# Strassen's seven block products for the second MLP product of a two-layer trunk on one core

## The chip, the cores and the metric

The kernel runs on one NeuronCore of a Trainium2 chip. Five engines work side by side, each through its own queue in order: PE (TensorE, matrix products into PSUM), DVE (VectorE), ACT (ScalarE), POOL (GpSimd) and SP (SyncE, which here issues every DMA). SBUF is the working memory of 128 partitions, PSUM holds eight banks of 128x512 float32 for the results of PE, DRAM holds inputs and spilled tensors. The metric is the device time of one execution in microseconds (us).

## The reference, cut to what matters

Two layers of a trunk over 1024 tokens with 1024 channels, in float32. Each layer has a token mixer, an output projection, and then an MLP with a hidden width of 4096:

```python
def sqrelu_mlp(h, w1, w2):
    return jnp.square(jax.nn.relu(h @ w1)) @ w2

for layer in range(2):
    h = rms_norm(x, norm_mix[layer])
    ...                                   # token mixer and memory attention
    x = x + jnp.concatenate([y_mix, y_mem], axis=-1) @ w_out[layer]
    x = x + sqrelu_mlp(rms_norm(x, norm_mlp[layer]), w_mlp_in[layer], w_mlp_out[layer])
```

The second MLP product is `hidden (1024x4096) @ w_mlp_out (4096x1024)`, added to the residual x.

## The kernel before

Everything is held transposed: channels on the partitions, tokens along the free axis, split into two halves `h` of 512 tokens. Each float32 operand of a product is split into a rounded part `hi` and a remainder `lo` (type float32r), and a product of 128x128 by 128x512 is three matmuls, hi·hi, hi·lo and lo·hi (`t3`). A weight block of 128x1024 is loaded by a DMA into one of two buffers `wr`, copied by ACT to `wh` (L242) and its remainder `wl` made by DVE or POOL (L244); there are three buffers each of `wh` and `wl`, and `wnext` prepares the plan's entries up to two ahead of the one in use.

The MLP of a layer is `mlp`. `mlp_z(m, hs)` makes 128 hidden channels for both token halves: 24 matmuls into a PSUM bank of tag `pj` (2 banks) by way of `mmq` (L269), then relu and scale on DVE (L849), the square's rounded part on ACT (L851), the square on POOL (L852) and its remainder on DVE (L853). The second product goes in eight groups `g` of four hidden blocks: for each of 8 output blocks `dm` and 2 halves, 12 matmuls (4 hidden blocks of three) into a `pj` bank by way of `mm` (L264), and one addition of that bank on DVE to the residual tile `x[h][dm]`, which stays in SBUF over the whole MLP (L900). A group so has 16 results of 12 matmuls, 192, and beside it stand 8 results of 24 matmuls, 192, for the next group's hidden blocks. In the last group of layer 0, x is also stored to DRAM (`xs`, in the profile `xspill`), squared and summed for the next norm (`sqacc`, L322 and L328), and its first half split for the next layer (`split`, L333 and L334). In the last group of layer 1 the tiles go to `out`; the very last tile is done in two halves of 256.

SBUF is shared out by hand: `R` has 58 tiles of 128x512 for split operands, `F` has 25 tiles of 128x515 for everything in float32; both hand out the tile that has been free the longest. The order of the instructions on each engine is not that of the code: a scheduler of the language orders them when the program is built.

Of the kernel before, what the change touches and what calls it, by code (L numbers as in the profile page):

```python
# [139 lines left out]
class Builder:  # L140
    NR = 58
    NF = 25
# [3 lines left out]
    def __init__(self, ctx, tc, ins, out):  # L146
# [24 lines left out]
        self.plan = []  # L171
        self.wpos = self.wload = self.wrawn = 0
# [7 lines left out]
        self.hid = {}  # L180
# [5 lines left out]
        self.x = [None, None]  # L186
# [36 lines left out]

    def _wraw(self, upto):
        while self.wrawn < min(len(self.plan), upto):
            i = self.wrawn
            buf, src, n = self._wbuf(i, self.wraw), self.plan[i][0], self.plan[i][1]
            for s in (slice(0, n // 2), slice(n // 2, n)) if i == 0 else (slice(0, n),):
                self.nc.sync.dma_start(buf[:, s], src[:, s])
            self.wrawn += 1  # L230

    def _wsplit(self, upto):
        nc = self.nc
        while self.wload < min(len(self.plan), upto):
            i = self.wload
            self._wraw(i + 1)
            n = self.plan[i][1]
            parts = self.plan[i][2]
            raw, hi, lo = (self._wbuf(i, b) for b in (self.wraw, self.whi, self.wlo))
            for q in range(parts):  # L240
                s = slice(q * n // parts, (q + 1) * n // parts)
                nc.scalar.activation(hi[:, s], raw[:, s], AF.Copy)  # L242
                eng = nc.gpsimd if q in self.pool_parts else nc.vector
                eng.tensor_tensor(lo[:, s], raw[:, s], hi[:, s].bitcast(F32), ALU.subtract)  # L244
            self.wload += 1
            self._wraw(self.wload + 2)
# [497 lines left out]
    def outproj(self, h, ks, src, dst, gain, last):  # L744
        nc = self.nc
        if last and gain is not None:
            self.xg[h] = []
            self.x[h] = []
        for m in range(8):
# [14 lines left out]
            if last and gain is not None:  # L764
                self.xg[h].append(self.split(xv, self.pc(gain, m)))
                self.x[h].append(x)
            else:
                self.F.put(x)
# [4 lines left out]
    def outproj2(self, h, k0, k1, src, gain, side):  # L773
# [26 lines left out]
        self.x[h] = []  # L800
        for m in range(8):
# [7 lines left out]
            self.sqacc(m, h, xv, nc.vector)  # L809
            self.xg[h].append(self.split(xv, self.pc(gain, m)))  # L810
            self.x[h].append(x)
# [10 lines left out]

    def plan_mlp(self, l, nz, nw):
        w1 = [(self.ins["w1"][l * 32 + m], 1024, 1) for m in range(32)]
        w2 = [(self.ins["w2"][l * 32 + i], 1024, 1) for i in range(32)]
        self.plan += w1[nz:nz + nw] + w1[0:4]
        for g in range(8):
            self.plan += w1[4 * (g + 1):4 * (g + 1) + 2]
            self.plan += w2[4 * g:4 * g + 4]
            self.plan += w1[4 * (g + 1) + 2:4 * (g + 2)]  # L830

    def mlp_z(self, m, hs, hook=None):
        nc = self.nc
        wh, wl = self.wnext()
        for h in hs:
            if (m, h) in self.hid:
# [13 lines left out]
            hi, lo = self.R.get(), self.R.get()  # L850
            nc.scalar.activation(hi, r[:, n], AF.Square)  # L851
            nc.gpsimd.tensor_tensor(r[:, n], r[:, n], r[:, n], ALU.mult)  # L852
            nc.vector.tensor_tensor(lo, r[:, n], hi.bitcast(F32), ALU.subtract)  # L853
            self.F.put(r)
            self.hid[(m, h)] = (hi, lo)
# [5 lines left out]

    def mlp(self, l, src, nz, nw, nxt=None):
        nc = self.nc
        hid = self.hid
# [8 lines left out]
        self.x[0] = [self.load_x(k, 0, src) for k in range(8)]  # L873
        for g in range(8):
            if g < 7:
                for m in range(4 * g + 4, 4 * g + 6):
                    drain(self.mlp_z(m, (0, 1)))
# [7 lines left out]
            for c in range(4):  # L885
                wh, wl = self.wnext()
                for d in range(2):
                    dm = 2 * c + d
                    for h in range(2):
                        end = l == 1 and g == 7 and dm == 7 and h == 1  # L890
# [546 lines left out]
```

## Time and profile before

| | |
|---|---|
| three runs | 2275.31, 2278.61, 2284.72 us (median 2278.61) |
| the profiled execution's own time | 2282.31 us |
| its span, first to last instruction | 2280.6 us |
| mean granted TensorE clock | 0.988 |
| matmuls in the profile | 11058 |
| DMA over the span | 181.84 MB, mean 80 GB/s |

The profile is of one execution. A busy share is the time in which an engine had at least one instruction under way; matmuls overlap each other, so the time of one matmul row (395 ns) is longer than the pace at which they follow. "idle before" in a group's row is the time that the engine stood still just before such instructions, with what ended it.

### The profile page before, as it was taken

Reading aid. Unit: us, or ns where it says so; the run is one execution under the profiler, and the core shown is the slowest. Engines: PE = TensorE matmul, PEld = TensorE weight load, DVE = VectorE, ACT = ScalarE, POOL = GpSimd, SP = SyncE. Lnnn points to the kernel's source line nnn. Section 1 sums busy time; section 2 is a strip of 40 time slices with the busy share of each in tenths; the row PEclk is TensorE's granted clock in tenths of the full one; section 3 lists DMA queues with packets and bytes.
Section 4 is the critical chain, followed back from the end, with each engine's and each line's share of the span. In section 5 each row is a group of like instructions: output and inputs, shape, how many; then the busy total and the mean of one; then the engine's idle time right before and its main releaser. Section 6 shows DMA issues by size and latency. Waiting matters only on the chain.

```text
span 2280.6 us, 28820 instructions
## 1 busy us (share of the span) xinstructions
PE 2223.7 (98%) x11058; PEld 1852.9 (81%) x11058; DVE 1215.5 (53%) x2320; ACT 754.0 (33%) x1500; POOL 491.3 (22%) x504
## 2 busy tenths in 40 slices
PE   8889999999999999999999998999999999999999
PEld 6788777888888888888998996778788888888887
DVE  8988864333333333346677778887433333333332
ACT  5755642111111111124556756764211111111110
POOL 3743601110110110102133543321110110101100
PEclk9999999999999999999999998999999999999999
DMA  5422353111111111214335221564211111111112
GB/s 176 119 63 74 116 158 101 47 47 51 50 47 47 47 47 47 61 51 139 112 103 163 89 80 28 171 190 135 77 52 47 47 47 47 46 47 46 47 47 83
DMA packets 69785, 181.84 MB, mean 80 GB/s; under 512 B 7888, under 2 KB 10256, under 8 KB 69648
## 3 DMA queue, kind: packets, MB, share of 16 engines
q1 hardware_dynamic: 69648, 180.01, 25.9%
q8 instruction: 87, 1.43, 0.3%
q14 instruction: 50, 0.41, 0.1%
HBM read 162.12 MB, written 17.86 MB: 79 GB/s over the span
## 4 chain that ended last, share of the span: by engine, by line
PE 83%; DVE 9%; DMA 4%; ACT 2%; issue 2%; POOL 1%; SPq 0%; DVEq 0%; ACTq 0%; POOLq 0%
PE pspj L269 43%; PE pspj L264 31%; DVE wl L244 1%; DMA f<-xspill 1%; DMA xspill<-f 1%; PE pss L1072 1%; ACT f L209 1%; PE pss L264 1%; PE pspt L789 1%; PE pso L577 1%; PE pspt L1114 1%; DVE f L1077 1%; DVE r L340 1%; PE pspt L269 0%; PE pspj L789 0%
## 5 line engine op out<-in xcount | busy, mean ns | idle before, releaser
L269 PE MATMUL pspj<-r,wh 128*128 128x512 f32 x2656 | 849.8, 400 | 18.0 <-DVE f L759 9.7
L264 PE MATMUL pspj<-r,wh 128*128 128x512 f32 (+1 forms) x2056 | 644.2, 395 | 0.3 <-DVE f L900 0.3
L269 PEld LDWEIGHTS pspj<-r,wh 128*128 128x128 f32 x2656 | 499.2, 189 | 140.8 <-issue 7.7
L242 ACT ACTIVATE wh<-wr 128x256 fp32r<-128x256 f32 (+3 forms) x433 | 276.6, 669 | 905.9 <-PE pspj L264 421.9
L269 PE MATMUL pspj<-r,wl 128*128 128x512 f32 x1328 | 527.6, 397 | 0.0
L264 PEld LDWEIGHTS pspj<-r,wh 128*128 128x128 f32 x2056 | 385.3, 188 | 93.2 <-DVE f L900 0.8
L852 POOL TENSOR_TENSOR f<-f 128x512 f32<-128x512 f32 x128 | 166.9, 1304 | 1254.7 <-ACT r L851 1254.7
L264 PE MATMUL pspj<-r,wl 128*128 128x512 f32 (+1 forms) x1028 | 405.2, 394 | 0.0
L900 DVE TENSOR_TENSOR f<-f,pspj 128x512 f32<-128x512 f32 (+1 forms) x257 | 175.7, 684 | 422.6 <-PE pspj L264 422.5
L244 DVE TENSOR_TENSOR wl<-wr,wh 128x1024 fp32r<-128x1024 f32 (+3 forms) x322 | 287.4, 902 | 59.8 <-ACT wh L242 57.8
L269 PEld LDWEIGHTS pspj<-r,wl 128*128 128x128 f32 x1328 | 251.2, 189 | 60.3 <-issue 0.2
L269 PE MATMUL pspj<-wh,r 128*128 128x256 f32 (+1 forms) x1408 | 275.6, 289 | 5.7 <-DVE r L981 2.3
L849 DVE SCALAR_TENSOR_TENSOR f<-pspj,f 128x512 f32<-128x512 f32 x128 | 88.4, 691 | 282.0 <-PE pspj L269 279.5
L269 PEld LDWEIGHTS pspj<-wh,r 128*128 128x128 f32 x1408 | 226.7, 193 | 8.7 <-DVE r L981 2.6
L264 PEld LDWEIGHTS pspj<-r,wl 128*128 128x128 f32 x1028 | 193.1, 188 | 46.9
L269 PE MATMUL pspj<-wl,r 128*128 128x256 f32 (+1 forms) x704 | 201.8, 287 | 6.3 <-DVE wl L244 6.3
L851 ACT ACTIVATE r<-f 128x512 fp32r<-128x512 f32 x128 | 79.8, 624 | 289.4 <-DVE f L849 289.4
L853 DVE TENSOR_TENSOR r<-f,r 128x512 fp32r<-128x512 f32 x128 | 89.2, 697 | 149.5 <-POOL f L852 149.5
L269 PEld LDWEIGHTS pspj<-wl,r 128*128 128x128 f32 x704 | 135.6, 193 | 7.7 <-DVE wl L244 6.8
L244 POOL TENSOR_TENSOR wl<-wr,wh 128x256 fp32r<-128x256 f32 (+2 forms) x111 | 91.6, 849 | 123.4 <-ACT wh L242 115.7
L1089 POOL TENSOR_SCALAR f<-f,frc 128x512 f32<-128x512 f32 (+2 forms) x96 | 63.6, 672 | 150.2 <-DVE frc L1087 99.1
L209 ACT ACTIVATE f<-f,mn 128x512 f32<-128x512 f32 (+2 forms) x96 | 58.4, 611 | 31.4 <-DVE mn L1077 28.8
(246 smaller groups left out, 1987.9 us busy)
## 6 DMA issues: line engine op xcount, KB each, us to landing
wr<-in_w_dram SPq DMA_DIRECT2D x134, 512.0 KB, 3.6
f<-xspill SPq DMA_DIRECT2D x72, 256.0 KB, 3.6
xspill<-f SPq DMA_DIRECT2D x48, 256.0 KB, 2.2
f<-in_xT_dram SPq DMA_DIRECT2D x32, 256.0 KB, 3.5
wr<-in_wkv_dram SPq DMA_DIRECT2D x16, 512.0 KB, 3.7
wr<-in_wina_dram SPq DMA_DIRECT2D x15, 512.0 KB, 3.9
f<-cscr SPq DMA_DIRECT2D x24, 256.0 KB, 4.1
wr<-in_wxqa_dram SPq DMA_DIRECT2D x8, 512.0 KB, 3.7
```

The source lines that it names most:

```text
L209: i = self.nc.scalar.activation(*a, **k)
L242: nc.scalar.activation(hi[:, s], raw[:, s], AF.Copy)
L244: eng.tensor_tensor(lo[:, s], raw[:, s], hi[:, s].bitcast(F32), ALU.subtract)
L264: self.nc.tensor.matmul(out, lhsT=a, rhs=b, start=(j == 0), stop=(j == n - 1))
L269: self.nc.tensor.matmul(out, lhsT=a, rhs=b, start=(j == 0), stop=(j == n - 1))
L340: self.nc.vector.tensor_tensor(lo[:, :n], src, hi[:, :n].bitcast(F32), ALU.subtract)
L849: nc.vector.scalar_tensor_tensor(r[:, n], ps, 0.0, self.rsb[h][:, n], ALU.max, ALU.mult)
L851: nc.scalar.activation(hi, r[:, n], AF.Square)
L852: nc.gpsimd.tensor_tensor(r[:, n], r[:, n], r[:, n], ALU.mult)
L853: nc.vector.tensor_tensor(lo, r[:, n], hi.bitcast(F32), ALU.subtract)
L900: nc.vector.tensor_tensor(x, x, ps[:, cs], ALU.add)
L1089: nc.gpsimd.tensor_scalar(s[:, :n], s[:, :n], rc, 0.0, ALU.mult, ALU.add)
```

## The change

The second MLP product is cut into pairs: two output blocks by two hidden blocks by two token halves. Such a 2x2x2 piece has eight block products; in Strassen's form it has seven, p1 to p7, of sums and differences of blocks. The hidden blocks' sums (t1 to t4) are made by `hid_parts` in SBUF and all seven operands split into hi and lo; the weights' sums are made on POOL while the weight block is prepared, in two plan entries `s1` (blocks p1, p2, p6, p5) and `s2` (p7, p3, p4). Each product runs over the two pairs of a group, 6 matmuls to a PSUM bank, and `mlp_out` brings the seven banks together to four residual tiles. The residual tiles no longer stay in SBUF: they are loaded from `xspill` for each pair of output blocks in each group (`acc_load`) and stored again (`sink`), and the output projections ahead of the MLPs store x there too. `R` has 60 tiles and `F` 23. The weights of `w_mlp_out` are laid out by blocks on the host.

```diff
-    NR = 58
-    NF = 25
+    NR = 60
+    NF = 23
...
+    def _wpart(self, hi, lo, raw, eng):
+        self.nc.scalar.activation(hi, raw, AF.Copy)
+        eng.tensor_tensor(lo, raw, hi.bitcast(F32), ALU.subtract)
...
+                if parts == "s1":
+                    self.wx = f
+                    G.tensor_tensor(f[:, q:2 * q], a21, a22, ALU.add)
+                    G.tensor_tensor(f[:, 0:q], f[:, q:2 * q], a11, ALU.subtract)
+                    self._wpart(hi[:, 0:512], lo[:, 0:512], raw[:, 0:512], nc.vector)
+                    self._wpart(hi[:, 512:1024], lo[:, 512:1024], f[:, 0:512], nc.vector)
+                else:
+                    G.tensor_tensor(f[:, 0:q], a11, a21, ALU.subtract)
+                    G.tensor_tensor(f[:, q:2 * q], a12, self.wx[:, 0:q], ALU.subtract)
+                    self._wpart(hi[:, 512:768], lo[:, 512:768], a22, nc.vector)
+                    self._wpart(hi[:, 0:512], lo[:, 0:512], f[:, 0:512], nc.vector)
...
-            hi, lo = self.R.get(), self.R.get()
-            nc.scalar.activation(hi, r[:, n], AF.Square)
             nc.gpsimd.tensor_tensor(r[:, n], r[:, n], r[:, n], ALU.mult)
-            nc.vector.tensor_tensor(lo, r[:, n], hi.bitcast(F32), ALU.subtract)
-            self.F.put(r)
-            self.hid[(m, h)] = (hi, lo)
+            self.zz[(m, h)] = r
...
+    def hid_parts(self, m):
...
+        p["b11"] = self.split_sb(b11)
+        V.tensor_tensor(b11, b12, b11, ALU.subtract)
+        p["t1"] = self.split_sb(b11)
+        p["b21"] = self.split_sb(b21)
+        p["b22"] = self.split_sb(b22)
+        V.tensor_tensor(b12, b22, b12, ALU.subtract)
+        p["t3"] = self.split_sb(b12)
+        V.tensor_tensor(b11, b22, b11, ALU.subtract)
+        p["t2"] = self.split_sb(b11)
+        V.tensor_tensor(b21, b21, b11, ALU.subtract)
+        p["t4"] = self.split_sb(b21)
...
+    def acc_load(self, q):
+        return {(a, b): self.load_x(2 * q + a, b, self.xs) for a in range(2) for b in range(2)}
...
+        def sink(a, b):
+            f = acc[(a, b)]
+            x, dm = f[:, n], 2 * q + a
+            if g == 7 and l == 1:
+                nc.sync.dma_start(self.out[dm, :, b * H:(b + 1) * H], x)
+            else:
+                nc.sync.dma_start(self.xs[dm, :, b * H:(b + 1) * H], x)
+            if g == 7 and l == 0:
+                self.sqacc(dm, b, x, V if b == 0 else None)
+                if b == 0:
+                    self.xg[0].append(self.split(x, self.pc("gmix1", dm)))
+            self.F.put(f)
+
+        for q in range(4):
...
+            p1 = self.psum("pj")
+            prod(p1, 0, w, "b11")
+            nc.scalar.activation(t, p1, AF.Copy)
+            V.tensor_tensor(c11, c11, p1, ALU.add)
+            p2 = self.psum("pj")
+            prod(p2, 1, w, "b21")
+            V.tensor_tensor(c11, c11, p2, ALU.add)
+            sink(0, 0)
+            p6 = self.psum("pt")
+            prod(p6, 2, w, "t2")
+            V.tensor_tensor(t, t, p6, ALU.add)
+            p5 = self.psum("s")
+            prod(p5, 3, w, "t1")
+            V.tensor_tensor(u, t, p5, ALU.add)
+            G.tensor_tensor(c12, c12, u, ALU.add)
+            G.tensor_tensor(c22, c22, u, ALU.add)
...
+            p7 = self.psum("s")
+            prod(p7, 0, w, "t3")
+            V.tensor_tensor(t, t, p7, ALU.add)
+            V.tensor_tensor(c22, c22, p7, ALU.add)
+            G.tensor_tensor(c21, c21, t, ALU.add)
...
+            p3 = self.psum("pt")
+            prod(p3, 1, w, "b22")
+            V.tensor_tensor(c12, c12, p3, ALU.add)
+            sink(0, 1)
+            sink(1, 1)
+            p4 = self.psum("pt")
+            prod(p4, 2, w, "t4")
+            V.tensor_tensor(c21, c21, p4, ALU.add)
+            sink(1, 0)
...
         for g in range(8):
+            if g:
+                parts = []
+                for m in range(4 * g + 1, 4 * g + 4):
+                    drain(self.mlp_z(m, (0, 1)))
+                    if m % 2:
+                        parts.append(self.hid_parts(m - 1))
+            acc = self.acc_load(0)
             if g < 7:
-                for m in range(4 * g + 4, 4 * g + 6):
-                    drain(self.mlp_z(m, (0, 1)))
+                drain(self.mlp_z(4 * g + 4, (0, 1)))
...
-                        for cs in (slice(0, 256), slice(256, 512)) if end else (slice(0, H),):
-                            ps = self.psum("pj")
-                            terms = []
-                            for kk in range(4):
-                                s = slice(kk * M + d * P, kk * M + (d + 1) * P)
-                                a, b = hid[(4 * g + kk, h)]
-                                terms += self.t3(wh[:, s], wl[:, s], a[:, cs], b[:, cs])
-                            self.mm(ps[:, cs], terms)
-                            x = self.x[h][dm][:, cs]
-                            nc.vector.tensor_tensor(x, x, ps[:, cs], ALU.add)
+            self.mlp_out(l, g, parts, acc)
```

Because a scheduler sets the order, two places are shown on DVE. The first is in the middle of an MLP, where one group's second product ends and the next hidden blocks begin. Before, L900 is the addition of a bank, L244 a weight remainder, L849 and L853 belong to the hidden blocks:

```order
L900 TENSOR_TENSOR f_130<-f_130,pspj_4754 128x512
L900 TENSOR_TENSOR f_126<-f_126,pspj_4768 128x512
L900 TENSOR_TENSOR f_125<-f_125,pspj_4782 128x512
L900 TENSOR_TENSOR f_139<-f_139,pspj_4796 128x512
L244 TENSOR_TENSOR wl_154<-wr_149,wh_151 128x1024
L849 SCALAR_TENSOR_TENSOR f_148<-pspj_4813,f_132 128x512
```

Now the same place holds the eight additions of seven banks (L949 and L952 for p1 and p2, L956 for p6, L959 for p5, L967 and L968 for p7, L973 for p3, L978 for p4), the weight remainder (L246), and `hid_parts` of the next group (L372 a remainder, L896 a difference):

```order
L372 TENSOR_TENSOR r_123<-f_128,r_122 128x512
L949 TENSOR_TENSOR f_127<-f_127,pspj_5013 128x512
L896 TENSOR_TENSOR f_128<-f_139,f_128 128x512
L952 TENSOR_TENSOR f_127<-f_127,pspj_5022 128x512
L956 TENSOR_TENSOR f_132<-f_132,pspt_5031 128x512
L372 TENSOR_TENSOR r_83<-f_128,r_82 128x512
L959 TENSOR_TENSOR f_131<-f_132,pss_5039 128x512
L246 TENSOR_TENSOR wl_155<-wr_149,wh_152 128x1024
L967 TENSOR_TENSOR f_132<-f_132,pss_5052 128x512
L973 TENSOR_TENSOR f_142<-f_142,pspt_5062 128x512
L968 TENSOR_TENSOR f_130<-f_130,pss_5052 128x512
L978 TENSOR_TENSOR f_135<-f_135,pspt_5072 128x512
```

Between two additions of banks now stand instructions that read two tiles of SBUF, and the banks have three tags (`pj`, `pt`, `ps` with tag `s`) in place of one.

The second place is the last group of layer 0, where the residual is also prepared for the next layer. Before, on DVE (L328 adds squares, L334 splits x for layer 1):

```order
L900 TENSOR_TENSOR f_135<-f_135,pspj_7095 128x512
L244 TENSOR_TENSOR wl_155<-wr_150,wh_152 128x256 x2
L900 TENSOR_TENSOR f_130<-f_130,pspj_7121 128x512
L328 TENSOR_TENSOR f_145<-f_145,f_132 128x512
L334 SCALAR_TENSOR_TENSOR r_91<-f_130,par,r_90 128x512
L900 TENSOR_TENSOR f_126<-f_126,pspj_7140 128x512
```

Now (L360 adds squares, L366 splits x):

```order
L978 TENSOR_TENSOR f_129<-f_129,pspt_7776 128x512
L246 TENSOR_TENSOR wl_156<-wr_149,wh_153 128x256
L360 TENSOR_TENSOR f_126<-f_126,f_136 128x512
L973 TENSOR_TENSOR f_138<-f_138,pspt_7856 128x512
L967 TENSOR_TENSOR f_133<-f_133,pss_7846 128x512
L366 SCALAR_TENSOR_TENSOR r_93<-f_129,par,r_92 128x512
L360 TENSOR_TENSOR f_126<-f_126,f_127 128x512
L246 TENSOR_TENSOR wl_154<-wr_150,wh_151 128x512
L968 TENSOR_TENSOR f_143<-f_143,pss_7846 128x512
L949 TENSOR_TENSOR f_140<-f_140,pspj_7890 128x512
L956 TENSOR_TENSOR f_141<-f_141,pspt_7912 128x512
```

The additions of the squares and the splits stand between additions of banks on which the next products wait for a free bank.

More of the change, by code (lines that the diff above doesn't have):

```diff
@@ L222, in _wbuf, with _wridx, _wrawbuf @@
         return bufs[i % len(bufs)][:, :self.plan[i][1]]
+    def _wridx(self, i):
+        while len(self.ridx) <= i:
+            e = self.plan[len(self.ridx)]
+            self.nraw += e[0] is not None
+            self.ridx.append(self.nraw - 1)
+        return self.ridx[i]
+    def _wrawbuf(self, i):
+        return self.wraw[self._wridx(i) % len(self.wraw)]
     def _wraw(self, upto):
@@ new lines, in acc_load, with mlp_out, prod @@
+    def acc_load(self, q):
+        return {(a, b): self.load_x(2 * q + a, b, self.xs) for a in range(2) for b in range(2)}
+    def mlp_out(self, l, g, parts, acc):
+        nc = self.nc
+        V, G = nc.vector, nc.gpsimd
+        n = slice(0, H)
+        def prod(ps, blk, w, key):
+            terms = []
+            for p in range(2):
+                c = slice(blk * M + p * P, blk * M + (p + 1) * P)
+                terms += self.t3(w[0][:, c], w[1][:, c], *parts[p][key])
+            for j, (a, b) in enumerate(terms):
+                nc.tensor.matmul(ps, lhsT=a, rhs=b, start=(j == 0), stop=(j == 5))
+            if q == 3:
+                for p in range(2):
+                    self.R.put(*parts[p][key])
+        def sink(a, b):
[3 more added lines that the diff above has]
+                nc.sync.dma_start(self.out[dm, :, b * H:(b + 1) * H], x)
+            else:
+                nc.sync.dma_start(self.xs[dm, :, b * H:(b + 1) * H], x)
[4 more added lines that the diff above has]
+            self.F.put(f)
+        for q in range(4):
+            c11, c12, c21, c22 = (acc[(a, b)][:, n] for a in range(2) for b in range(2))
+            w = self.wnext()
+            tf, uf = self.F.get(), self.F.get()
+            t, u = tf[:, n], uf[:, n]
+            p1 = self.psum("pj")
[14 more added lines that the diff above has]
+            G.tensor_tensor(c22, c22, u, ALU.add)
+            self.F.put(uf)
+            nxt = self.acc_load(q + 1) if q < 3 else None
+            w = self.wnext()
+            p7 = self.psum("s")
[3 more added lines that the diff above has]
+            G.tensor_tensor(c21, c21, t, ALU.add)
+            self.F.put(tf)
+            p3 = self.psum("pt")
[7 more added lines that the diff above has]
+            sink(1, 0)
+            acc = nxt
@@ L872, in mlp @@
             drain(self.mlp_z(m, (0, 1), step))
[L873 removed]
+            if m == 1:
+                parts = [self.hid_parts(0)]
+        parts.append(self.hid_parts(2))
         for g in range(8):
+            if g:
[5 more added lines that the diff above has]
+            acc = self.acc_load(0)
             if g < 7:
[L876 to L877 removed]
+                drain(self.mlp_z(4 * g + 4, (0, 1)))
             else:
```

83 lines of the change are left out of this document (35 added, 48 removed).

## The prediction

> **What bounds the kernel now.** I read the page's first part, then the chain of work that ended last in the MLP, then the stages' windows, then the groups by line inside an MLP. The first part says which engine is full:
>
> ```profile
> PE 2223.7 (98%) x11058; PEld 1852.9 (81%) x11058; DVE 1215.5 (53%) x2320; ACT 754.0 (33%) x1500; POOL 491.3 (22%) x504
> ```
>
> A share of 98% could hide waits, so the chain is read next, from 380 to 800 us, in layer 0's MLP. Its columns are start, length, engine, tile, line and count; the first line sums the chain's shares.
>
> ```profile
> by line: PE pspj L269 52.2%; PE pspj L264 47.8%
> ...
> 419.99 44.80 PE pspj L264 x192
> 464.79 44.80 PE pspj L269 x192
> ```
>
> The chain is PE alone: 192 matmuls of the second product (L264), 192 of the next hidden blocks (L269), 44.80 us each, so 44.80 / 192 = 233.3 ns a matmul. The results of 12 matmuls and those of 24 go at the same pace, so ending a result costs nothing visible. The windows show the same by stage (PE, PEld, DVE, ACT, POOL busy, granted clock, DMA share, GB/s):
>
> ```profile
> 0.00:380.00 380.00, 347.01 (x1806) 292.36 (x1807) 309.42 (x579) 210.08 (x419) 149.93 (x142) 0.96 0.39 119
> 379.86:1024.79 644.93, 644.93 (x2765) 518.86 (x2765) 230.94 (x295) 99.88 (x128) 77.32 (x60) 1.00 0.17 49
> 1300.00:1600.00 300.00, 282.20 (x1616) 241.58 (x1615) 232.57 (x578) 181.85 (x414) 97.72 (x129) 0.96 0.39 120
> ```
>
> In the MLP PE is never idle at a granted clock of 1.00, and DVE is busy 230.94 / 644.93 = 36% of the time. Only the first 380 us and the stretch from 1300 us on have PE idle (33 and 18 us).
>
> **What the change removes.** Four output pairs by seven products of 6 matmuls are 168 matmuls in a group where 192 stood. Two layers of eight groups: 16 x 24 = 384 matmuls, each on the chain, at 233.3 ns: **-89.6 us**. The Trainium skill (TensorE: Matmul & The Clock Gate, Part 1) gives 215.7 ns from start to start for 512 columns at full clock; by it the saving would be 82.8 us; the row is slower than the page, and the measurement decides. The last tile's two halves of 256 columns cost about what one of 512 does, and are left at nothing.
>
> **What it adds, and beside what.** The prices come from these groups (busy, then mean ns of one); the first six are of the MLP window alone, the others of the whole span:
>
> ```profile
> L900 DVE TENSOR_TENSOR f<-f,pspj 128x512 f32<-128x512 f32 x111 | 76.2, 687 | 188.1 <-PE pspj L264 188.1
> L244 DVE TENSOR_TENSOR wl<-wr,wh 128x1024 fp32r<-128x1024 f32 x52 | 63.7, 1225 | 10.7 <-ACT wh L242 10.7
> L853 DVE TENSOR_TENSOR r<-f,r 128x512 fp32r<-128x512 f32 x49 | 33.9, 691 | 60.4 <-POOL f L852 60.4
> L849 DVE SCALAR_TENSOR_TENSOR f<-pspj,f 128x512 f32<-128x512 f32 x49 | 33.9, 691 | 114.2 <-PE pspj L269 114.2
> L852 POOL TENSOR_TENSOR f<-f 128x512 f32<-128x512 f32 x49 | 63.9, 1304 | 479.8 <-ACT r L851 479.8
> L851 ACT ACTIVATE r<-f 128x512 fp32r<-128x512 f32 x49 | 30.6, 624 | 121.7 <-DVE f L849 121.7
> ...
> L244 DVE TENSOR_TENSOR wl<-wr,wh 128x512 fp32r<-128x512 f32 x47 | 33.5, 715 | 11.7 <-ACT wh L242 10.1 <-PE pspt L789 1.3
> L244 DVE TENSOR_TENSOR wl<-wr,wh 128x256 fp32r<-128x256 f32 x114 | 55.8, 513 | 10.4 <-ACT wh L242 10.1
> L244 POOL TENSOR_TENSOR wl<-wr,wh 128x256 fp32r<-128x256 f32 x98 | 81.3, 852 | 116.1 <-ACT wh L242 114.8 <-POOL f L1089 1.0
> ```
>
> A group (360 matmuls, 84.0 us of PE) then asks of DVE: 32 additions of banks at 687 ns (22.0), four times three remainders of 512 or 256 columns, 2 x 715 + 715 + 513 (10.6), four remainders of 1024 (4.9), eight L849-like (5.5), and for `hid_parts` 14 remainders and 8 differences at 691 (15.2): 58.2 us. Of POOL: 12 additions (15.6) and 8 squares (10.4) at 1304 ns, 16 sums of weights at 852 (13.6): 39.7 us. ACT gets some 16 + 4 + 14 copies at 624 ns or less and four of a whole block, under 30 us. All of it is beside 84.0 us of PE. In the second product alone PE needs 39.2 us; DVE has its 22.0 of banks, of the order rows ahead five half-entries and three whole weight blocks and two rows of `hid_parts` (about 11.6): 33.6 us. That is near, but PE does not wait for the newest addition: a bank of `pj`, `pt` or `s` comes back one output pair (42 matmuls, 9.8 us) after it was last used. Working one group through by hand, row by row in the order shown, the additions finish about 5 us before their bank is asked for again, and a weight entry 6 us or more before its first matmul. With POOL holding DVE up by one of its instructions (1.3 us) the cover stays. I take **+3 us** for all 16 groups; the bounds are nothing and one POOL instruction of 1.3 us a group, 21 us.
>
> The residual now costs 8 MB of DMA a group, beside 4 MB of weights: 12 MB in 84 us, 143 GB/s, where the window above shows 49. These are the issues, with the size and the time to landing, and the page's traffic in 40 slices:
>
> ```profile
> wr<-in_w_dram SPq DMA_DIRECT2D x134, 512.0 KB, 3.6
> f<-xspill SPq DMA_DIRECT2D x72, 256.0 KB, 3.6
> xspill<-f SPq DMA_DIRECT2D x48, 256.0 KB, 2.2
> f<-cscr SPq DMA_DIRECT2D x24, 256.0 KB, 4.1
> ...
> GB/s 176 119 63 74 116 158 101 47 47 51 50 47 47 47 47 47 61 51 139 112 103 163 89 80 28 171 190 135 77 52 47 47 47 47 46 47 46 47 47 83
> ```
>
> The page's slices reach 190 GB/s, with loads of 256 KB landing in 4.1 us at most by median. A pair's tiles are asked for an output pair (9.8 us) ahead. SP holds them in one queue, stores and loads mixed, so a store that waits for its addition holds the weight load behind it; the weight buffer it fills is wanted some 10 us later. I cost it at nothing; without that cover it is the second rival.
>
> **The end of layer 0** is denser. From the last hidden blocks on, DVE has 32 additions (22.0), ten rows of `hid_parts` (6.9), 18 remainders of weights (11.0), two L849-like (1.4), and of work that stood there already about 16 us, by these rows (the first four columns as above):
>
> ```profile
> L334 DVE SCALAR_TENSOR_TENSOR r<-f,par,r 128x512 fp32r<-128x512 f32 x64 | 52.3, 822 | 16.9 <-ACT r L333 16.9
> L328 DVE TENSOR_TENSOR f<-f,f 128x512 f32<-128x512 f32 x25 | 17.7, 708 | 3.0 <-ACT f L322 2.4
> L444 DVE SCALAR_TENSOR_TENSOR r<-f,par,r 128x256 fp32r<-128x256 f32 x16 | 11.6, 764 | 2.6 <-ACT r L443 2.6
> ```
>
> (In the changed order six of them at 822 ns, seven at 708, eight at 764: 16.0 us.) Together about 57 us, while PE has 5.6 (the last hidden block), 39.2, and 48 matmuls of 256 columns of the memory projection, which the scheduler puts between. Such matmuls go at 119 ns, by this piece of the chain after that stage:
>
> ```profile
> 1095.98 4.04 PE pspj L269 x34
> ```
>
> 48 x 0.119 = 5.7, so PE has 51 us. DVE becomes the bound for this group. 57 - 51 = 6, and something for waits: **+7 us**; from nothing (later PE work covers the backlog) to 57 - 39 = 18. Layer 1's last group has no such extras (about 36 us of DVE against 39.2), but nothing hides `hid_parts` after the last hidden block except products that do not need it: **+2 us**, 0 to 6.
>
> **The tail.** Before, half a tile is added after the last matmul (L900 of 256 columns) and stored. Now POOL's last addition waits for DVE's of p7 and DVE's last for POOL: about 0.7 + 1.3 + 0.7 us with 1.4 of them beside p4's matmuls, then a store of 256 KB: **+1.5 us**, 1 to 3.
>
> **The other stages** keep their work but not their order, and two tiles of `F` fewer. While the code is laid out the free list falls to 1 where it fell to 3, in the first layer's projections and in the attention, where PE is already idle 33 and 18 us. A shorter list means that a tile is asked for sooner after its last use; a wait of 1.3 us at a few places: **+3 us**; as the scheduler shuffles these stages either way, -6 to +12.
>
> **The sum**, against the profiled execution's own 2282.3 us (span 2280.6): 2282.3 - 89.6 + 3 + 7 + 2 + 1.5 + 3 = 2209.2. That execution lies 3.7 us above the median of the three runs, 2278.61, which spread over 9.4; I say **2208 us**.
>
> **Rivals.**
>
> *DVE and POOL hold each other up (slower).* DVE instructions that read two SBUF tiles are stretched here, those that read a bank are not (min, median, max in ns; the third line is the group, with its mean):
>
> ```profile
> L340 DVE TENSOR_TENSOR r<-pspt,r x48: 660/681/693, 156.6 to 1362.5; 128x512 fp32r<-128x512 f32 x48
> L340 DVE TENSOR_TENSOR r<-f,r x26: 674/680/1454, 22.0 to 1559.4; 128x512 fp32r<-128x512 f32 x26
> ...
> L340 DVE TENSOR_TENSOR r<-f,r 128x512 fp32r<-128x512 f32 x26 | 19.3, 743 | 1.1 <-ACT r L339 1.1
> ```
>
> The change gives DVE 30.7 us a group of two-tile work and POOL 39.7 us. If DVE lost all of POOL's time it would need 58.2 + 39.7 = 97.9 us where the group of before took 89.6: 16 x 8.3 = +133, **2415 us**. It costs something from 84.0 - 58.2 = 25.8 us of loss a group, and makes the kernel slower from 31.4. Against it: the row's median is unchanged at 680, its mean rises to 743 only, and the two kinds of work add to 70 us, within 84. The Trainium skill (SBUF — State Buffer, "Who interferes with whom") says that a DVE instruction with two SBUF inputs and a GpSimd instruction that reads SBUF exclude each other for their whole length; by that rule alone the 70 us are one after the other, and still fit; the two rows agree with it. Chance 4%.
>
> *The DMA queue.* Each output pair waits for its tiles or the weight behind a store. If loads land in 7.2 us in place of 3.6 and a pair's cover is missed by a fifth of that four times a group, 16 x 4 x 0.7 = 45 us: **2253 us**. For it: 143 GB/s is three times what stood there. Against it: 190 GB/s elsewhere with landings of 4.1. Chance 9%.
>
> *Short results cost PE.* 448 products end after 6 matmuls. A matmul lasts 395 ns and follows at 233:
>
> ```profile
> L264 PE MATMUL pspj<-r,wh 128*128 128x512 f32 (+1 forms) x2056 | 644.2, 395 | 0.3 <-DVE f L900 0.3
> ```
>
> If each product's start lost that overlap, 448 x 0.162 = 73 us go back: **2282 us**, no change, so the eighth product would be gone and its time not. Against it: results of 12 and of 24 at the same 44.80. Chance 3%.
>
> *Other stages lose more.* The first 380 us and the attention take +20 in place of +3: **2225 us**. Chance 12%.
>
> **How the numbers follow.** The forecast has the remaining 72%. Its own bounds, all terms low: 2282.3 - 89.6 - 6 + 1 = 2188; for the high end the sum with the DMA rival's half or the other stages' 20 and layer 0's 18: 2236. So 2188 to 2236, which leaves out the first and third rivals and part of the second. About 0.5% (11 us) is what a measurement of this kernel can tell from no change: faster by more than that 93% (forecast, second and fourth rival), within it 3% (the third), slower 4% (the first).
>
> **What would show it.** In the changed profile: about 10,660 matmuls; in the chain, pieces of 168 and 192 at 39.2 and 44.8 us, PE's idle in the MLP windows near nothing and clock 1.00; DVE near 70% busy and POOL near 47% there; PE waiting in the last group of layer 0 for additions of banks (L959, L968, L978), a few us in all; a span outside the MLPs within 12 us of before. Wrong if a group takes over 86 us, if PE waits for `wl`, `f` or a DMA in each group, or if the early stages grow.

## The result, and the profile after

| | before | after |
|---|---|---|
| median of the runs (4 each) | 2280.07 us (2275.31 to 2284.72) | 2215.28 us (2212.54 to 2218.49) |
| profiled execution, own time | 2282.31 us | 2215.74 us |
| its span | 2280.6 us | 2214.1 us |
| matmuls in the profile | 11058 | 10662 |

The ratio after to before is 0.9716, 95% interval 0.9692 to 0.9741. The forecast was 2208 us with a range of 2188 to 2236, so the time lies in it, 7 us above the forecast. Of all executions below, one (of the kernel with half seven, half eight products) took 6470.95 us, where its others took 2200.80 to 2204.14; its ratio leaves that one out.

These are rows of the page of the changed kernel: busy time and share of each engine, and three DMA issues with their size and their median time to landing.

```profile
PE 2138.4 (97%) x10662; PEld 1780.2 (80%) x10662; DVE 1617.9 (73%) x2991; ACT 932.4 (42%) x1852; POOL 983.2 (44%) x952
...
f<-xspill SPq DMA_DIRECT2D x312, 256.0 KB, 3.0
xspill<-f SPq DMA_DIRECT2D x288, 256.0 KB, 3.0
wr<-in_w_dram SPq DMA_DIRECT2D x134, 512.0 KB, 4.1
```

DVE's time rose by a third and POOL's doubled; the residual's 312 loads land in 3.0 us by median, the 72 of before in 3.6; the weights take 4.1 in place of 3.6. To see where the time went, the span is cut at two places that both programs have: the first product of layer 0, and the first matmul of the long piece of projections behind layer 0's MLP (231 matmuls of L269 before; of L301 after, where the trace holds 227 of them). Before makes two more hidden results ahead of its first product, 11.2 us, so its cut lies that much earlier than the product. These are the windows of before at these cuts, and last its end of layer 0 (from the last hidden result on):

```profile
0.00:408.63 408.63, 375.64 (x1928) 315.39 (x1929) 318.79 (x591) 215.14 (x426) 156.18 (x147) 0.96 0.37 114
408.63:1099.99 691.36, 691.19 (x3092) 561.83 (x3090) 274.53 (x428) 132.65 (x206) 85.24 (x67) 1.00 0.20 59
1099.99:2280.60 1180.61, 1156.90 (x6043) 975.72 (x6041) 622.14 (x1302) 406.24 (x868) 249.93 (x290) 0.99 0.26 80
1024.79:1100.00 75.21, 75.04 (x452) 66.10 (x450) 52.98 (x145) 37.82 (x86) 14.16 (x12) 1.00 0.45 141
```

And the windows of the changed kernel (columns: window, length, PE, PEld, DVE, ACT and POOL busy, granted clock, DMA share, GB/s): the same three, then four groups of layer 0 in full pace, six of layer 1, layer 1's last products, the end of layer 0, and two pieces of it.

```profile
0.00:411.62 411.62, 376.13 (x1928) 315.33 (x1929) 327.24 (x607) 220.34 (x435) 157.18 (x157) 0.96 0.38 119
411.62:1076.21 664.59, 652.38 (x2903) 529.58 (x2902) 466.42 (x748) 215.80 (x374) 327.82 (x281) 0.99 0.47 153
1076.21:2214.10 1137.89, 1109.84 (x5835) 935.24 (x5833) 824.22 (x1636) 496.26 (x1044) 498.22 (x514) 0.99 0.43 138
411.70:746.90 335.20, 335.20 (x1441) 270.25 (x1440) 223.11 (x328) 96.84 (x152) 166.75 (x144) 1.00 0.46 151
1638.50:2136.90 498.40, 497.75 (x2138) 401.09 (x2137) 337.06 (x494) 145.09 (x228) 251.55 (x217) 1.00 0.47 153
2170.60:2209.50 38.90, 38.90 (x168) 31.13 (x166) 34.12 (x50) 11.02 (x19) 22.55 (x19) 1.00 0.42 147
987.40:1076.21 88.81, 76.60 (x431) 65.35 (x430) 79.27 (x180) 44.98 (x102) 39.07 (x31) 0.94 0.49 157
1017.90:1021.60 3.70, 0.22 (x1) 0.00 (x1) 3.70 (x4) 0.44 (x2) 3.63 (x3) 1.00 0.21 71
1021.60:1025.60 4.00, 4.00 (x11) 3.19 (x12) 4.00 (x7) 2.08 (x4) 3.01 (x3) 0.61 0.26 91
```

Each layer should lose 192 matmuls, 44.8 us. Ahead of the MLP the changed kernel takes 411.62 - 408.63 = 3.0 us more. Layer 0's MLP takes 664.59 where 691.36 - 44.8 = 646.6 were due: 18.0 more. The rest, with layer 1, takes 1137.89 where 1135.8 were due: 2.1 more, of which 1.0 is the tail. Together 23.1 of the 89.6 us are given back, and 18.0 of them at one place. That place is not the groups: there PE is busy 335.20 of 335.20 us at a clock of 1.00, and in layer 1 all but 0.65 of 498.40. It is the end of layer 0, 88.81 us long with PE idle for 12.2 and the clock at 0.94. The waits of PE there (engine, tile and line, what it waited for; us, times, longest) say for whom:

```profile
PE pss L923 <- DVE f L968: 3.5, 1, 3.5
PE pspj L301 <- DVE f L448: 2.4, 1, 2.4
PE pspj L301 <- DVE r L520: 1.7, 1, 1.7
PE pspj L923 <- DVE f L949: 1.2, 1, 1.2
PE pspj L301 <- DVE f L949: 1.1, 1, 1.1
PE pspt L923 <- ACT f L948: 1.0, 1, 1.0
PE pspt L923 <- DVE wl L246: 0.9, 1, 0.9
PE pspt L923 <- DVE f L956: 0.3, 1, 0.3
```

Nearly all is DVE, and no line names a DMA. DVE's groups from 985 to 1050 us (busy, mean ns of one, idle before):

```profile
L246 DVE TENSOR_TENSOR wl<-wr,wh 128x256 fp32r<-128x256 f32 x18 | 11.4, 656 | 2.7 <-ACT wh L245 2.7
L366 DVE SCALAR_TENSOR_TENSOR r<-f,par,r 128x512 fp32r<-128x512 f32 x7 | 7.5, 1072 | 1.3 <-ACT r L365 1.3
L360 DVE TENSOR_TENSOR f<-f,f 128x512 f32<-128x512 f32 x6 | 7.0, 1160 | 0.0
...
L959 DVE TENSOR_TENSOR f<-f,pss 128x512 f32<-128x512 f32 x4 | 2.7, 677 | 0.0
```

Instructions that read a PSUM bank (L959) keep 677 ns. Those that read two SBUF tiles take much longer than the rows of before from which the prediction was priced: 1072 ns for the remainders of the split (822 before), 1160 for the sums of squares (708 before). POOL is busy in 39.07 of these 88.81 us, against 14.16 of 75.21 before. These means mix two kinds, as the order in time shows. DVE (start, length, line) through PE's longest wait, from 1017.9 to 1021.6 us:

```profile
1017.51 1.76 DVE L360 TENSOR_TENSOR f<-f,f 128x512 f32<-128x512 f32 x1
1019.20 1.75 DVE L246 TENSOR_TENSOR wl<-wr,wh 128x512 fp32r<-128x512 f32 x1
1020.87 0.68 DVE L968 TENSOR_TENSOR f<-f,pss 128x512 f32<-128x512 f32 x1
```

And POOL beside it:

```profile
1017.01 1.72 POOL L969 TENSOR_TENSOR f<-f,f 128x512 f32<-128x512 f32 x1 [2.16 <-DVE f L967]
1018.69 1.71 POOL L360 TENSOR_TENSOR f<-f,f 128x512 f32<-128x512 f32 x1
```

DVE's L360 starts while POOL's L969 is under way and ends 0.54 us after it; L246 starts while POOL's L360 is under way and ends 0.55 us after that. Only then does L968 free the bank for which PE waits. The timeline lists 28 instructions of 128x512 on two SBUF tiles one by one in this stretch: 18 take 0.68 to 0.76 us, and each of the ten longer ones ends 0.54 or 0.55 us after a POOL instruction that had started before it.

### The profile page after: what moved, and what is told of

Read it like the earlier page. It is cut to its first block, busy times and chain, and to the rows that moved or that the text cites. A ratio compares the mean times of both kernels' runs of the same rounds, so it can differ in the third digit from the quotient of the medians.

```text
span 2214.1 us, 31106 instructions
## 1 busy us (share of the span) xinstructions
PE 2138.4 (97%) x10662; PEld 1780.2 (80%) x10662; DVE 1617.9 (73%) x2991; ACT 932.4 (42%) x1852; POOL 983.2 (44%) x952
## 5 line engine op out<-in xcount | busy, mean ns | idle before, releaser
L301 PE MATMUL pspj<-r,wh 128*128 128x512 f32 x2656 | 845.8, 398 | 15.5 <-ACT wh L245 5.6
L301 PEld LDWEIGHTS pspj<-r,wh 128*128 128x128 f32 x2656 | 498.4, 189 | 137.3 <-ACT wh L245 5.6
L301 PE MATMUL pspj<-r,wl 128*128 128x512 f32 x1328 | 528.4, 398 | 0.2 <-DVE wl L246 0.2
L246 DVE TENSOR_TENSOR wl<-wr,wh 128x256 fp32r<-128x256 f32 (+2 forms) x386 | 303.7, 794 | 67.7 <-ACT wh L245 66.7
L301 PEld LDWEIGHTS pspj<-r,wl 128*128 128x128 f32 x1328 | 251.2, 189 | 60.9 <-DVE wl L246 0.7
L301 PE MATMUL pspj<-wh,r 128*128 128x256 f32 (+1 forms) x1408 | 275.5, 290 | 15.2 <-ACT f L450 5.1
L372 DVE TENSOR_TENSOR r<-f,r 128x512 fp32r<-128x512 f32 x250 | 190.3, 773 | 132.8 <-ACT r L371 132.6
L923 PE MATMUL pspt<-r,wh 128*128 128x512 f32 x768 | 246.8, 395 | 1.2 <-ACT f L948 1.0
L301 PEld LDWEIGHTS pspj<-wh,r 128*128 128x128 f32 x1408 | 225.9, 193 | 19.8 <-ACT f L450 6.0
L301 PE MATMUL pspj<-wl,r 128*128 128x256 f32 (+1 forms) x704 | 201.8, 288 | 5.0 <-DVE wl L246 5.0
L960 POOL TENSOR_TENSOR f<-f,f 128x512 f32<-128x512 f32 x64 | 96.3, 1505 | 230.8 <-DVE f L959 218.5
L923 PEld LDWEIGHTS pspt<-r,wh 128*128 128x128 f32 x768 | 144.1, 188 | 36.5 <-ACT wh L245 1.4
L923 PE MATMUL pss<-r,wh 128*128 128x512 f32 x512 | 161.6, 396 | 3.5 <-DVE f L968 3.5
L923 PE MATMUL pspj<-r,wh 128*128 128x512 f32 x512 | 161.2, 396 | 1.4 <-DVE f L949 1.2
L923 PE MATMUL pspt<-r,wl 128*128 128x512 f32 x384 | 152.4, 397 | 0.9 <-DVE wl L246 0.9
L246 POOL TENSOR_TENSOR wl<-wr,wh 128x256 fp32r<-128x256 f32 (+2 forms) x111 | 89.7, 831 | 132.5 <-ACT wh L245 129.0
L301 PEld LDWEIGHTS pspj<-wl,r 128*128 128x128 f32 x704 | 135.5, 193 | 6.7 <-DVE wl L246 5.8
L245 ACT ACTIVATE wh<-f 128x512 fp32r<-128x512 f32 x128 | 80.4, 630 | 143.2 <-PE pspj L923 61.3
```

What stands on the lines that cost most here:

```text
L245: self.nc.scalar.activation(hi, raw, AF.Copy)
L246: eng.tensor_tensor(lo, raw, hi.bitcast(F32), ALU.subtract)
L301: self.nc.tensor.matmul(out, lhsT=a, rhs=b, start=(j == 0), stop=(j == n - 1))
L372: self.nc.vector.tensor_tensor(lo[:, :n], src, hi[:, :n].bitcast(F32), ALU.subtract)
L923: nc.tensor.matmul(ps, lhsT=a, rhs=b, start=(j == 0), stop=(j == 5))
L960: G.tensor_tensor(c12, c12, u, ALU.add)
```

## The experiments

The first measure is the time of the runs; the second the length of the end of layer 0, from the end of its last hidden result to the long piece of projections (75.2 us before with 24 more matmuls, 88.8 after). The kernels were run on several occasions, each time beside the kernel before (third column); the changed kernel was not run again, so times of different occasions are compared by their ratios. Each length is from one execution. The kernel with twelve more additions leaves this stretch as it is in the change, and has it 3.3 us longer: differences of that size say little.

| kernel | median, us | before beside it, us | ratio to before, 95% | end of layer 0, us |
|---|---|---|---|---|
| the change | 2215.28 | 2280.07 | 0.9716 (0.9692 to 0.9741) | 88.8 |
| last group of layer 0 with eight products | 2198.22 | 2277.94 | 0.9652 (0.9635 to 0.9668) | 74.9 |
| eight products everywhere, residual streamed | 2286.18 | 2277.94 | 1.0035 (1.0022 to 1.0049) | - |
| the same, F of 25 tiles | 2284.00 | 2277.94 | 1.0023 (1.0010 to 1.0037) | - |
| without GpSimd's additions there | 2200.10 | 2277.94 | 0.9658 (0.9642 to 0.9674) | 75.3 |
| GpSimd's additions awaited by nobody | 2209.76 | 2275.57 | 0.9707 (0.9694 to 0.9720) | 84.1 |
| VectorE makes GpSimd's additions | 2214.99 | 2275.57 | 0.9733 (0.9720 to 0.9745) | 91.8 |
| twelve more GpSimd additions a group | 2220.96 | 2275.57 | 0.9759 (0.9745 to 0.9773) | 92.1 |
| last group half seven, half eight | 2203.00 | 2275.57 | 0.9680 (0.9668 to 0.9692) | 80.4 |
| seven VectorE additions fewer there | 2206.27 | 2275.94 | 0.9690 (0.9674 to 0.9707) | 84.0 |

### Eight products in the last group of layer 0

```diff
+                if l == 0 and g == 7:
+                    self.plan += [(self.ins["w2"][(l * 8 + g) * 4 + q], 1024, 1)]
...
+        if l == 0 and g == 7:
+            for q in range(4):
+                w = self.wnext()
...
+                        for p in range(2):
+                            for i in range(2):
+                                blk = ((0, 1), (3, 2))[a][i]
+                                c = slice(blk * M + p * P, blk * M + (p + 1) * P)
+                                terms += self.t3(w[0][:, c], w[1][:, c], *parts[p][f"b{i + 1}{b + 1}"])
+                        self.mm(ps, terms)
+                        x = acc[(a, b)][:, n]
+                        V.tensor_tensor(x, x, ps, ALU.add)
+                        sink(a, b)
```

The four hidden blocks of each pair are split as they are, in place of the seven operands of `hid_parts`.

> The last group of layer 0 alone goes back to eight block products (192 matmuls, 16 bank additions on VectorE in place of 32, no sums of blocks on GpSimd or VectorE there). TensorE gets 24 x 233.3 ns = 5.6 us more. Theory A (VectorE is the bound at the end of layer 0): VectorE has some 21 us less there, so the 18 us lost there fall to 3 or less; net -9 us, about 2206 us. Theory B (the loss comes from late loads of the next stage's weights and from the memory stage that shares this place, not from the new additions): the loss stays above 12 us and the 5.6 come on top: 2215 to 2221 us.

Measured: 2198.22 us (2198.07 to 2200.93), faster than both kernels. The window of its end of layer 0:

```profile
986.40:1061.25 74.85, 74.85 (x451) 66.15 (x450) 52.77 (x145) 38.39 (x85) 11.20 (x10) 1.00 0.50 163
```

PE is never idle and the clock is 1.00, although 24 matmuls more stand there. POOL is busy 11.20 us, and DVE's L366 and L360 take 752 and 693 ns. The memory stage (`kv`) and its weight loads are still in this place, so theory B falls; theory A holds, and by more than it said: all of the loss goes. The stretch without loss is thus 74.85 - 5.6 = 69.2 us for seven products, and the change lost 88.8 - 69.2 = 19.6 there. (The 18.0 above is the same loss, counted over the whole MLP of layer 0, where some matmuls of the next stage lie on the other side of the cut.) The profiled spans differ by 2214.1 - 2196.5 = 17.6 us: 14.0 in the stretch, 1.0 ahead of it and 2.6 behind it. By the ratios the two kernels differ by about 14.6.

### The streamed residual alone, with two sizes of the pool

```diff
-                self.plan += [(self.ins["w2"][(l * 8 + g) * 4 + q], 1024, "s1"), (None, 768, "s2")]
+                if True:
+                    self.plan += [(self.ins["w2"][(l * 8 + g) * 4 + q], 1024, 1)]
```

and the loop of the run before it in every group. The second kernel has, besides, `NR = 58` and `NF = 25`.

> Eight block products in every group, everything else of the change kept (residual streamed once per group, squares on GpSimd, F of 23 tiles and R of 60). All 384 matmuls come back. If the streaming is hidden and only the other stages pay for the smaller pool: 2280 + 3 to 5 = 2283 to 2286 us, ratio 1.001 to 1.003 to the kernel before, TensorE never idle in the MLP. If streaming has a cost of its own that the MLP's pace hid: over 2291 us.

> As the run before it, with F of 25 tiles and R of 58 as in the kernel before. If the smaller pool costs the 3 us that the stage ahead of layer 0's MLP lost: that stage is 3 us shorter again, the whole 3 to 5 us less. If the loss there is only another order of the same work: within 2 us of the run with 23 tiles, or on the other side.

Measured: 2286.18 and 2284.00 us, where the kernel before had 2277.94 beside them. The steady groups of the first, and PE's only wait from 940 to 1112 us:

```profile
412.00:995.00 583.00, 583.00 (x2502) 469.86 (x2502) 224.36 (x260) 86.80 (x102) 51.00 (x49) 1.00 0.44 143
```

```profile
PE pspj L301 <- DVE f L965: 4.5, 1, 4.5
```

143 GB/s of residual and weights hide behind PE in each steady group. The streaming and the smaller pool cost 2286.18 - 2277.94 = 8 us in all, none of it in the steady groups. The one wait, 4.5 us, stands at the end of layer 0, and the profile leads it back to the streaming: L965 stands on DVE behind a row of the memory stage (L476), which waits 7.1 us for ACT; and ACT stands idle 7.6 and 3.2 us in front of two squares (L479), till stores of the residual (`xspill<-f`) have ended and their tiles of `F` are free. (In the changed kernel ACT waits 10.2 us before these squares for such stores, with no wait of PE behind them.) With 25 tiles PE waits 1.8 us for POOL's L481 of the memory stage there and 1.6 for L965. Ahead of the MLP the first product starts at 413.44 us with 23 tiles and at 405.31 with 25 (408.63 in the kernel before, by the same cut). But the second kernel gives most of that back in the attention, and the medians differ by 2.2 us: neither of the two expectations fits. Whether the 3 us that the change lost ahead of layer 0's MLP are the pool's, or of another order of the same work, stays open.

### Without GpSimd's additions in the last group

```diff
-                self.sqacc(dm, b, x, V if b == 0 else None)
+                if b == 0 or dm == 0:
+                    self.sqacc(dm, b, x, V)
...
-            G.tensor_tensor(c12, c12, u, ALU.add)
-            G.tensor_tensor(c22, c22, u, ALU.add)
+            if not (l == 0 and g == 7):
+                G.tensor_tensor(c12, c12, u, ALU.add)
+                G.tensor_tensor(c22, c22, u, ALU.add)
...
-            G.tensor_tensor(c21, c21, t, ALU.add)
+            if not (l == 0 and g == 7):
+                G.tensor_tensor(c21, c21, t, ALU.add)
```

> Seven products everywhere; in the last group of layer 0 GpSimd's additions of u, u and t to c12, c22 and c21 are left out (12 instructions) and so are the squares of tiles 1 to 7 of the second token half with their additions (7 more on GpSimd, 7 on ScalarE); VectorE's work is the same. Theory A1 (the two engines hold each other up): VectorE's instructions on two SBUF tiles (L360, L366, L246) fall from 1.16, 1.07, 0.66 us to near 0.75, 0.75, 0.45, its busy time there falls by 8 us or more, the 18 us lost there to 8 or less: about 2205 us. Theory A2 (VectorE is the bound by its plain load, held up or not): busy falls by under 3 us, the loss stays at 14 or more: 2211 us or more.

Measured: 2200.10 us. Its end of layer 0, and three of DVE's groups there:

```profile
988.26:1063.54 75.28, 71.65 (x431) 63.84 (x430) 66.93 (x178) 40.30 (x95) 11.34 (x12) 0.98 0.57 185
```

```profile
L246 DVE TENSOR_TENSOR wl<-wr,wh 128x256 fp32r<-128x256 f32 x35 | 13.9, 414 | 2.1 <-ACT wh L245 2.1
L366 DVE SCALAR_TENSOR_TENSOR r<-f,par,r 128x512 fp32r<-128x512 f32 x8 | 5.9, 742 | 0.7 <-ACT r L365 0.7
L360 DVE TENSOR_TENSOR f<-f,f 128x512 f32<-128x512 f32 x7 | 4.8, 680 | 0.0
```

DVE's instructions are the same, and it is busy 12.3 us less (66.93 against 79.27). L360 falls from 1160 to 680 ns, L366 from 1072 to 742, L246 from 656 to 414 (over the whole stretch, 47 of them in each trace, from 511 to 416). The stretch is 13.5 us shorter. Theory A2 falls. What is left, 75.3 - 69.2 = 6 us, is an estimate of what DVE's plain load costs (seven squares on ACT are gone too). But this kernel also has nobody waiting for GpSimd's results, so the next one keeps GpSimd at work and is meant to take away only the waiting.

### GpSimd's additions awaited by nobody

```diff
-            G.tensor_tensor(c12, c12, u, ALU.add)
-            G.tensor_tensor(c22, c22, u, ALU.add)
+            last = l == 0 and g == 7
+            for c in (c12, c22):
+                G.tensor_tensor(u if last else c, u if last else c, u, ALU.add)
...
-            G.tensor_tensor(c21, c21, t, ALU.add)
+            G.tensor_tensor(t if last else c21, t if last else c21, t, ALU.add)
```

> Seven products everywhere; in the last group of layer 0 GpSimd's twelve additions stay as many and as long, but add u to u and t to t in place, so that c12, c22 and c21 lack them and no addition of VectorE waits for them. Squares are all there. If the engines hold each other up while both work (theory A1), nothing is gained: VectorE's two-tile instructions stay at 1.0 us and more there, the stretch from the last hidden blocks to the next stage stays within 4 us of the 88.7 of the changed kernel, 2211 us or more. If it was VectorE's waiting for GpSimd's results (theory A3), the stretch falls to 77 or less, about 2203 us, as in the run without the additions.

Measured: 2209.76 us, 84.1 us for the stretch.

```profile
987.84:1071.97 84.13, 74.67 (x431) 63.82 (x430) 77.89 (x178) 44.53 (x102) 34.03 (x31) 0.96 0.51 166
```

```profile
L246 DVE TENSOR_TENSOR wl<-wr,wh 128x256 fp32r<-128x256 f32 x21 | 13.3, 654 | 0.0
L366 DVE SCALAR_TENSOR_TENSOR r<-f,par,r 128x512 fp32r<-128x512 f32 x8 | 7.9, 989 | 0.7 <-ACT r L365 0.7
L246 DVE TENSOR_TENSOR wl<-f,wh 128x512 fp32r<-128x512 f32 x6 | 6.4, 1089 | 0.0
L360 DVE TENSOR_TENSOR f<-f,f 128x512 f32<-128x512 f32 x7 | 5.7, 817 | 0.0
```

Between the theories, nearer A1: the stretching stays for the most part (654, 989 and 1089 ns), DVE is busy 77.89 us (79.27 in the change, 66.93 without the additions), and 4.7 us go, a little more than the 4 that A1 allowed. By the ratios the time is no different from the change's. The 4.7 are not waits for GpSimd's results, for the changed kernel has none: these are DVE's additions to c22, c12 and c21 there, and the time that DVE stood idle before them is the last number.

```profile
L968 DVE TENSOR_TENSOR f<-f,pss 128x512 f32<-128x512 f32 x4 | 2.7, 676 | 0.0
L973 DVE TENSOR_TENSOR f<-f,pspt 128x512 f32<-128x512 f32 x4 | 2.7, 674 | 0.0
L978 DVE TENSOR_TENSOR f<-f,pspt 128x512 f32<-128x512 f32 x3 | 2.0, 680 | 0.0
```

DVE's only wait for POOL in the stretch is 0.9 us before L900, for a hidden block, and this kernel and the one without the additions have it too. So theory A3 falls. The twelve additions are as many here, but not as long: in place they read one tile and take 1152 and 1214 ns, where those of the change take 1512 to 1626, and POOL is busy 34.03 us in place of 39.07. How much of the 4.7 this makes, and how much is the spread between executions and orders, stays open.

### VectorE makes those additions

```diff
+        if l == 0 and g == 7:
+            G = V
```

> In the last group of layer 0 VectorE makes the twelve additions to c12, c22 and c21 in place of GpSimd. VectorE gets 12 x 0.68 = 8.2 us more. Plain load (A2): the stretch grows by about 8 us, 2223 us. Holding up (A1): GpSimd's 12 x 1.4 = 17 us there go, of which the run without them gave back 13 with the squares; some 8 to 10 of that come back, so the 8.2 are paid for: 2212 to 2217 us, no difference from the changed kernel, with L360, L366 and L246 shorter.

Measured: 2214.99 us, no different from the changed kernel within the intervals. The stretch is 3.0 us longer, though DVE got 8.2 us more work; L246 fell to 497 ns and L360 to 682. The window of the stretch:

```profile
987.82:1079.65 91.83, 74.36 (x428) 63.12 (x426) 79.36 (x188) 45.10 (x102) 19.55 (x19) 0.96 0.47 150
```

With twelve additions more DVE is busy no longer than in the change (79.36 us against 79.27): what they cost, POOL's lighter load gives back. This agrees with A1 and not with A2. The stretch itself is weak evidence: the next kernel leaves this group as it was, and its stretch is 3.3 us longer too.

### Twelve more additions on GpSimd in each other group

```diff
             G.tensor_tensor(c22, c22, u, ALU.add)
+            if g < 7:
+                for _ in range(2):
+                    G.tensor_tensor(u, u, u, ALU.add)
...
             G.tensor_tensor(c21, c21, t, ALU.add)
+            if g < 7:
+                G.tensor_tensor(t, t, t, ALU.add)
```

> Twelve more additions in place (u to u, t to t) on GpSimd in each of the 14 groups that are not a layer's last: 12 x 1.3 = 16 us a group, GpSimd from about 44% to 65% in the MLP; u, t and what is computed from t after them are wrong. Price of holding up where VectorE has slack: VectorE has 84 - 58 = 26 us a group. If only overlapping instructions are stretched, VectorE gets up to 10 us busier a group and TensorE still never waits: the pieces stay at 39.2 and 44.8, 2215 to 2220 us. If the whole of GpSimd's time is lost to VectorE (the first rival of the prediction), 58 + 40 + 16 = 114 us a group, 14 x 30 = +420 us.

Measured: 2220.96 us for 168 more instructions, about 220 us of GpSimd. (In this kernel nothing reads u and t after these additions.) Four steady groups of it, and two of DVE's groups in that window:

```profile
411.70:746.90 335.20, 334.38 (x1434) 268.57 (x1433) 239.45 (x327) 94.54 (x151) 228.43 (x192) 1.00 0.45 151
```

```profile
L372 DVE TENSOR_TENSOR r<-f,r 128x512 fp32r<-128x512 f32 x56 | 47.0, 851 | 43.6 <-ACT r L371 43.6
L246 DVE TENSOR_TENSOR wl<-f,wh 128x512 fp32r<-128x512 f32 x32 | 31.4, 980 | 0.0
```

The same two of the changed kernel in the same window:

```profile
L372 DVE TENSOR_TENSOR r<-f,r 128x512 fp32r<-128x512 f32 x56 | 42.2, 764 | 37.6 <-ACT r L371 37.6
L246 DVE TENSOR_TENSOR wl<-f,wh 128x512 fp32r<-128x512 f32 x32 | 24.1, 754 | 0.4
```

In four groups POOL is busy 61.7 us more (228.43 - 166.75) and DVE 16.3 more (239.45 - 223.11), a quarter of it. PE is idle 0.8 us in four groups. Where DVE has slack, the holding up costs next to nothing, even at a POOL share of 68%; the prediction's first rival was far off. By the ratios the kernel is some 10 us slower than the change, and the intervals do not meet; the two profiled spans differ by 3.7 us, 3.3 of them at the end of layer 0. What makes up the rest is not shown.

### Half of the last group with eight products

The first two output pairs with seven, the last two with eight. For them b12 is split too, and the tiles of the MLP's input are given back one hidden block earlier:

```diff
+            if l == 0 and g == 7 and q >= 2:
+                w = self.wnext()
...
+                acc = nxt
+                continue
```

> In the last group of layer 0 the first two pairs of outputs by seven products and the last two by eight (180 matmuls there, 2.8 us fewer than with eight throughout). If VectorE and GpSimd catch up during the two plain pairs: 2.8 us less than the run with the whole last group plain, 2195 us. If the sums and the one more split of the seven products still bind: 2200 us or more, no better than that run.

Measured: 2203.00 us, 80.4 us for the stretch. It has 2.8 us of matmuls less than the kernel with eight throughout, and its stretch is 5.6 us longer all the same, 3.3 of it in one wait of PE for DVE (L968 here, an addition of a bank). The second expectation held: half of the group with seven products is no better than none.

### Seven VectorE additions fewer in the last group

```diff
-                self.sqacc(dm, b, x, V if b == 0 else None)
+                if b == 1 or dm == 0:
+                    self.sqacc(dm, b, x)
```

> Seven products everywhere, GpSimd as in the changed kernel; in the last group of layer 0 the squares of tiles 1 to 7 of the first token half are left out, with their seven additions on VectorE (L360, 1.16 us each there) and seven instructions on ScalarE. If VectorE's time is what the stretch waits for, all 7 x 1.16 = 8.1 us come back, between 5 (unstretched price, 7 x 0.68) and 8: from the end of the last hidden block to the next stage 80 to 84 us in place of 88.7. If GpSimd's queue is the bound there by itself, as the gain without its additions would also allow: within 2 us of 88.7.

Measured: 2206.27 us, 84.0 us for the stretch, 4.8 less:

```profile
988.33:1072.33 84.00, 75.00 (x436) 64.57 (x434) 75.92 (x171) 41.51 (x95) 37.73 (x31) 0.96 0.48 159
```

GpSimd's busy time hardly moves (37.73 against 39.07), so GpSimd's queue does not look like the bound by itself; the gain agrees with DVE's time as what the stretch waits for. Its size is that of the unstretched price, 7 x 0.68 = 4.8, not of 8.1: L366 stays at 1133 ns, so the work behind may meet GpSimd instead. But 4.8 is not far above the 3.3 us by which two stretches of the same work differ, and by the ratios (0.9690 and 0.9716) the time cannot be told from the change's.

## Why the prediction held, and the term that was too small

*The removed matmuls.* Right. 384 went, and each steady group takes 83.8 us with PE full (335.20 / 4).

*The steady groups, +3.* Nothing was lost there. DVE's 58.2 us a group were priced well (223.11 / 4 = 55.8 of busy time; the rows, which overlap a little, add up to 60.0), POOL's 39.7 too (41.7); the shares are 67% and 50% where 70 and 47 were named. The traffic was 151 GB/s where 143 were named: the sum took 12 MB a group, but 48 times 256 KB are 12.6 million bytes. The products of 6 matmuls go at the pace of the longer results, the loads land in 3.0 us, and the two engines' holding up is covered: three of the rivals are false, each by its own sign. The run with more work on GpSimd shows that the cover was wide.

*The end of layer 0, +7.* This is the term of the sum that was mis-sized: 18.0 measured, at its upper bound. The mechanism, that DVE becomes the bound for this group, was right: the run with eight products there loses nothing. The one with seven DVE additions fewer agrees, with 4.8 us. The step that failed is the pricing of DVE's 57 us at 708 to 822 ns, durations from a program in which POOL was mostly idle. With GpSimd's additions left out the stretch loses 6 us, about the 7 of the forecast. The rest, some 13.5 us, comes with POOL's twelve additions and seven sums of squares: DVE's same instructions are busy 12.3 us longer beside them, and the timeline shows why, a two-tile instruction that waits for a POOL instruction to end. DVE's waits for POOL's results are no part of it. The first rival's mechanism was thus real, but it cost time only at the one place where DVE has no slack. The sign that the prediction named came in part: PE waited for L968 (3.5 us), but also for L949 (2.3), and 4.1 us for the memory stage behind (L448, L520), not for L959 or L978.

*How the loss is made up on PE.* PE is idle for 12.2 of the 19.6 us. The other 7.4 lie inside its busy time, at a mean granted clock of 0.94; the prediction had no term for them. By that mean the clock would make 0.06 x 76.6 = 4.6 of them, an estimate. One gap is followed up below; what the rest is was not tried.

*Layer 1's last group, +2; the tail, +1.5; the other stages, +3.* Measured about 0 (PE is full from 2170.60 to 2209.50), 1.0, and 3.0 ahead of the MLP with 1.1 behind it. The fourth rival did not come. What of these few us is the smaller pool and what is chance of the order stays open: from the long piece of projections to the last matmul, the changed kernel takes 1133.3 us and the one with VectorE's additions, with the same instructions there, 1125.7.

*The sum.* 0 + 18.0 + 0 + 1.0 + 4.1 = 23.1 where 16.5 were taken; 6.5 us of error on 2209.2: one term 11 too low, and the others together 4.4 too high. That the whole came so near is in part luck.

## What to carry to other kernels

A trade of matmuls for additions pays where the other engines have slack, and should be left out where they have none: take the plain form in the one stage that is full, as the 2198 us kernel does. Find that stage by adding up VectorE's work stage by stage, and price its instructions on two SBUF tiles at the stretched durations that they will have beside GpSimd's new work, not at those of a program in which GpSimd is mostly idle. In this trace one that started beside a GpSimd addition took up to 1.78 us in place of 0.68 to 0.76.

## What the runs showed of the hardware

PE's granted clock was lower behind a gap. After 3.48 us without a matmul (the window from 1017.90 us above) the granted clock was 0.61 over the next 4 us, in which 11 matmuls started where 4.00 / 0.2333 = 17 fit. A stall of 3.5 us so cost about 5.

The Trainium skill (SBUF — State Buffer, "Who interferes with whom") has a VectorE instruction with two SBUF inputs and a GpSimd instruction that reads SBUF exclude each other. The runs agree on which instructions are stretched: L360, on two SBUF tiles, goes from 680 ns to 1160 with GpSimd's additions, L959, which reads a bank, stays at 677. They also show the waiting itself: the ten stretched instructions of 128x512 each end 0.54 or 0.55 us after a GpSimd instruction that had started before them. GpSimd waits in its turn: its addition at 1009.09 us, started just behind VectorE's L366 (1009.04 to 1009.78), takes 1.85 us, one at 1011.06 takes 1.29. So VectorE does not lose all of GpSimd's time: 16.3 of 61.7 us in the steady groups, and 12.3 of 27.7 (39.07 - 11.34) in the full stretch.
